# Turning two sets of tiles on TensorE and letting the framework's timeline simulation order the queues, in a hybrid attention and RWKV-7 layer

## The chip, the cores and the metric

The kernel runs on one core of one Trainium2 chip. The time is device microseconds of one execution, the median of several runs. The kernel before took 1992.68 us (three runs, 1992.07 to 1992.70).

## The reference

One layer over 256 tokens and 4096 features, all in float32. A wide projection feeds 16 heads of forgetting attention, 32 heads of RWKV-7 and a gate; one output projection and a LayerNorm follow.

```
proj = x @ w_in                              # 256 x 4096 by 4096 x 16.6k
fox:   p = softmax(q k^T / sqrt(128) + c_t - c_s, causal);  fox_out = p v
rwkv:  S_t = S_{t-1} diag(decay_t) + (S_{t-1} a_t) b_t^T + v_t k_t^T;  y_t = S_t r_t
h   = concat(fox_out, groupnorm(y) * g + b + bonus) * silu(z)
out = LayerNorm(2^(1/4) * x + h @ w_out)
```

## The kernel before

**Projections.** The input projection is cut into 8 groups n of 4 blocks b, each of 512 columns: a group holds two fox heads and two pairs of RWKV heads, the output projection has 8 more blocks of 512 columns. Per block 16 weight tiles w{n}_{b}_{q} of 128x1024 come by DMA. ACT casts each to a rounded upper part (w_qh, L140), DVE subtracts it to get the rest (w_ql, L141), and TensorE multiplies three times per 128 rows of the contraction: L146 and L147 with the upper part, L148 with the rest. One weight tile feeds 12 matmuls of 128x512. In the first and the last weight tile of a block the two accumulators acc{n}_{b}_0 and acc{n}_{b}_1 are filled one behind the other, otherwise in turn. Three such accumulators lie in PSUM, five more PSUM tiles (`pst`) serve everything else. The output projection does the same in L860 to L862.

**Side work.** Everything else is written as generators, each of which runs on to its next `yield` at every `slot()` between projection matmuls. So the program order strews this work among the projections, and `wait(W[...])` says how many slots a generator lets pass. For group n the RWKV generator (`rwkv`) builds BK (the keys and removal vectors per chunk), the small triangular blocks gb and lt, sends the diagonal ones out and loads them back spread over the partitions (nd, Nb), solves them row by row in 31 pairs of DVE instructions (prod L579, xc L582), and then goes over 4 chunks in a chain of small matmuls: rh, copied to R, up, copied to UV by ACT, sp (which reads BKt, the turned BK), added to SV by DVE. The fox generator (`fox`) makes the logits lg, their softmax, turns the probabilities into pT, multiplies them with vt (fop, L744 and L745) and copies that to fo (ACT L747). The two heads of a group use vt{n}, which ACT copies out of the block 1 accumulators (L912), so fop of the odd head has to be done before vt of the next group is written.

**How tiles are turned before.** A 128x128 turn is done in two halves: DVE transposes 32x32 squares in place (STREAM_TRANSPOSE), four DMAs of `turn` (L281) write the tile to DRAM in an order that moves the squares, and one DMA loads it back. BK takes two DVE transposes, four DMAs and one load per group (L547 and `turns`), lg of heads 0 to 13 one DVE transpose, four DMAs and one load. Heads 14 and 15 already have their probabilities turned by three TensorE transposes with the identity (L739) and an ACT copy out of PSUM (L740).

**What sets the order.** The framework's scheduler places all instructions in its queues by priority and readiness. Some have to keep the program's order (`tc.keep_in_program_order`), among them the DMAs of `issue` and some DVE transposes. Engines work their queues strictly in order. At the end of the program the LayerNorm of the first 128 tokens is finished among the last projections of the second 128: zp0 (a transpose of the row factors), eight matmuls wp0_0 to wp0_7 (L1010), each followed by a DVE update of 512 columns (L1011); then the statistics of the second half, mv1 (L979), and its eight updates.

Of the kernel before, what the change touches and what calls it, by code (L numbers as in the profile page):

```python
# [10 lines left out]
F32 = mybir.dt.float32  # L11
# [6 lines left out]
P = 128  # L18
# [3 lines left out]
G = 16  # L22
C = 64
NCH = S // C
# [60 lines left out]
def layer(ctx: ExitStack, tc: tile.TileContext, xt, xtok, w_lora, w_main, muv, w_o, up, par, mulora, fbias, lng, lnb, cst, out):  # L85
    nc = tc.nc
# [8 lines left out]
    def pst(name):  # L95
        return ps.tile([P, 512], F32, tag="ps", name=name)
# [34 lines left out]
    ident = cs[:, C_ID : C_ID + P]  # L131
    ones = cs[:, C_ONES : C_ONES + P]

    def column(name, i):
        return prm[:, PAR.index(name), i : i + 1]
# [21 lines left out]
    for n, (k0, k1) in enumerate(pieces):  # L157
        for k in range(k0, k1):
            t = xpool.tile([P, 2, S], F32R, tag=f"x{k}", name=f"x{k}")
# [31 lines left out]
    def wait(n):  # L191
        for _ in range(n):
            yield
# [67 lines left out]
    rp = mid.enter_context(tc.tile_pool(name="rp", bufs=1))  # L261
# [6 lines left out]
    def t256(tag, name, bufs=1):  # L268
        return rp.tile([P, S], F32, tag=tag, name=name, bufs=bufs)
# [10 lines left out]
    def issue(out, src):  # L280
        tc.keep_in_program_order(nc.sync.dma_start(out=out, in_=src))  # L281

    def turn(src, name, each=2):
        _, m, cols = src.shape
        d = dram.tile([cols // B, B, m, 4, B], F32, tag=f"dt{m}_{cols}", name=name, bufs=2)
        s = src.rearrange("p m (q t) -> p m q t", t=B)
        for a in range(4):
            issue(d[:, :, :, a, :].rearrange("q i m t -> i m q t"), s[B * a : B * (a + 1)])
            if a % each == each - 1:
                yield  # L290
        return d
# [79 lines left out]
    def gate(y, key, k):  # L371
        far = k < FAR
        while len(storing) > 1:
            yield
        h = rp.tile([P, S], F32, tag="h", name=f"h{k}")
        nc.vector.scalar_tensor_tensor(h, y, 0.5, szs[key], ALU.mult, ALU.mult)
        pool, tag, bufs = (rp, "hl", 2) if far else (xpool, f"x{k}", 1)
        hl = pool.tile([P, 2, S], F32R, tag=tag, name=f"hl{k}", bufs=bufs)
        nc.scalar.copy(hl[:, 0, :], h)
        nc.vector.tensor_tensor(hl[:, 1, :], h, hl[:, 0, :].bitcast(F32), ALU.subtract)  # L380
        if far:
            storing.append(k)
            yield from wait(SENT)
            issue(hd[k], flat(hl).bitcast(F32))
            kept_h.add(k)
            storing.remove(k)
        else:
            ht[k] = hl
# [6 lines left out]
    def flat(t):  # L395
        return t.rearrange("p a b -> p (a b)")
# [108 lines left out]
    def rwkv(n):  # L505
# [3 lines left out]
        q = pairs[n]  # L509
        lc, BK, lt, bon = q["lc"], q["BK"], q["lt"], q["bon"]  # L510
# [9 lines left out]
        p, t = bks[n], vs_[n]  # L520
# [22 lines left out]
        SV = [rp.tile([P, 2, NCH, C], F32, tag=f"SV{j}", name=f"SV{j}_{n}") for j in range(2)]  # L543
        UV = [rp.tile([P, 2, NCH, C], F32, tag=f"UV{j}", name=f"UV{j}_{n}") for j in range(2)]
        yield from wait(W["tp"])
        for u in range(2):
            tc.keep_in_program_order(nc.vector.transpose(flat(BK[:, u]), flat(BK[:, u])))  # L547
        yield from wait(W["d1"])
        BKt = rp.tile([P, 2, NCH, P], F32, tag="shl", name=f"BKt{n}")

        def turns():
            d = yield from turn(BK.rearrange("p u c t -> p (u c) t"), f"BKt{n}", 1)
            yield from wait(2)
            issue(BKt.rearrange("p u c t -> p (u c t)"), d.rearrange("q i g a t -> (q i) (g a t)"))
            yield
            vst = UV[0].rearrange("p u c v -> p (u c v)").rearrange("p (m q) -> p m q", m=2)
            for a in range(2):
                tc.keep_in_program_order(nc.vector.transpose(vst[:, a, :], vs_[n][:, a, :]))
            yield from wait(3)
            d = yield from turn(vst, f"vt{n}", 1)  # L560
            yield from wait(2)
            vv[n] = rp.tile([P, 2, S], F32, tag="s2", name=f"vv{n}")
            issue(vv[n], turned_back(d))
            yield from wait(4)
            nc.vector.tensor_tensor(flat(bon), flat(bon), flat(vv[n]), ALU.mult)
            for u in range(2):
                nc.scalar.activation(bon[:, u], bon[:, u], AF.Identity, bias=column("gn_bias", i0 + u))
            bonned.add(n)

        other = turns()  # L570
        prod = rp.tile([P, 2, NJ, B], F32, tag="prod", name=f"prod{n}")
        xc = rp.tile([P, 2, NJ, B], F32, tag="xc", name=f"xc{n}")
# [39 lines left out]
        for u in range(2):  # L612
            for c in range(NCH):
                for j in range(2):
                    a, b = slice(C * j, C * j + B), slice(C * j + B, C * j + C)
# [17 lines left out]
        for u in range(2):  # L633
            for c in range(NCH):
                for j in range(2):
                    a, b = slice(C * j, C * j + B), slice(C * j + B, C * j + C)
                    nc.tensor.matmul(xp[a, u * P + c * B : u * P + (c + 1) * B], Q[b, u, c, :], X[b, u, c, C * j + B : C * j + C], start=True, stop=True)
        for j in range(2):
            a = slice(C * j, C * j + B)
# [67 lines left out]
    def fox(i, q, k, vt):  # L707
        nb = rp.tile([P, 3, P], F32, tag="nb", name=f"nb{i}")
        row = ncd[i : i + 1, :]
        nc.sync.dma_start(out=flat(nb[:, 0:1, :]), in_=row[:, :P].to_broadcast([P, P]))  # L710
        nc.sync.dma_start(out=flat(nb[:, 1:3, :]), in_=row.to_broadcast([P, S]))
        for m in (0, 2):
            nc.gpsimd.affine_select(out=nb[:, m, :], in_=nb[:, m, :], compare_op=ALU.is_ge, fill=NEG, base=0, pattern=[[-1, P]], channel_multiplier=1)
        yield from wait(W["fs"])
        sp = pst(f"fsp{i}")
        nc.tensor.matmul(sp[:, :P], q[:, :P], k[:, :P], start=True, stop=True)
        nc.tensor.matmul(sp[:, P : 3 * P], q[:, P:], k, start=True, stop=True)
        lg = rp.tile([P, 3, P], F32, tag="lg", name=f"lg{i}")
        spv = sp[:, : 3 * P].rearrange("p (a t) -> p a t", t=P)
        st = rp.tile([P, 6], F32, tag="fst", name=f"fst{i}", bufs=2)  # L720
        for m, blk in enumerate((slice(0, 1), slice(1, 3))):
            nc.vector.scalar_tensor_tensor(lg[:, blk, :], spv[:, blk, :], ct[:, m * NF + i : m * NF + i + 1], nb[:, blk, :], ALU.add, ALU.add)
            nc.vector.tensor_reduce(st[:, m : m + 1], lg[:, blk, :], AX.XY, ALU.max, negate=True)
            nc.scalar.activation(lg[:, blk, :], lg[:, blk, :], AF.Exp, bias=st[:, m : m + 1], accum_out=st[:, 2 + m : 3 + m])
            nc.vector.reciprocal(st[:, 4 + m : 5 + m], st[:, 2 + m : 3 + m])
            nc.vector.tensor_scalar(lg[:, blk, :], lg[:, blk, :], st[:, 4 + m : 5 + m], None, ALU.mult)
        if i < G - 2:
            nc.vector.transpose(flat(lg), flat(lg))
        yield from wait(W["fp"])
        if i < G - 2:  # L730
            ld = yield from turn(lg, f"fpt{i}")
            yield
        pT = rp.tile([P, 3 * P], F32, tag="nb", name=f"pT{i}")
        if i < G - 2:
            issue(pT, ld.rearrange("q i m a t -> (q i) (m a t)"))
        else:
            pt = pst(f"fpt{i}")
            for m in range(3):
                nc.tensor.transpose(pt[:, m * P : (m + 1) * P], lg[:, m, :], ident)  # L739
            nc.scalar.copy(pT, pt[:, : 3 * P])  # L740
        yield from wait(W["fo"])
        op = pst(f"fop{i}")
        f = slice(i % 2 * P, i % 2 * P + P)
        nc.tensor.matmul(op[:, :S], vt[:, 0, f], pT[:, :S], start=True, stop=False)  # L744
        nc.tensor.matmul(op[:, P:S], vt[:, 1, f], pT[:, S:], start=False, stop=True)  # L745
        o = t256("fq", f"fo{i}")
        nc.scalar.copy(o, op[:, :S])  # L747
        while f"f{i}" not in szs or 2 * i >= FAR and not closed:
            yield
        yield from gate(o, f"f{i}", 2 * i)  # L750
        foxed.add(i)
# [6 lines left out]
    def chain():  # L758
        while not ff:
            yield  # L760
        yield from forget()
        for n in range(G // 2):
            yield from rwkv(n)
# [5 lines left out]
    def turned_back(d):  # L769
        return d.rearrange("(u b) i m a t -> u (b i) (m a t)", b=4).rearrange("u p s -> p u s")  # L770
# [5 lines left out]
    def unload(n, b, bk, vt):  # L776
# [43 lines left out]
        else:  # L820
# [4 lines left out]
            yield from wait(LAND - 1)  # L825
        nc.scalar.mul(fq, fq, FOX_SCALE)
        side(fox(i, fq, fk, vt))
        yield
        silu2(zf, f"f{i}")
# [89 lines left out]
    for b, q in outs:  # L919
        if q == 0:  # L920
            pool, tag = (ps, "ps") if b == 1 or b and b % 2 == 0 else (pp, "pp")
# [91 lines left out]
    z0, _, last = moments(0)  # L1013
# [79 lines left out]
```

## Time and profile before

| | before |
|---|---|
| median of the runs, us | 1992.68 |
| profiled execution, span, us | 1990.4 |
| TensorE busy, instructions | 1948.0 us, 10063 |
| VectorE busy | 1384.1 us |
| ScalarE busy | 962.3 us |
| DMA, share of 16 engines on the main queue | 72.3% |

The page states the span of the profiled execution and no further time of its own; the runs' median lies 2.28 us above this span, for what comes ahead of the first and behind the last instruction. TensorE is busy 98% of the span, so the time is read from TensorE's gaps and from the pace between them. A timeline row has start, duration, engine, line, operation and, in brackets, how long the engine had been idle before it and what ended the idle time. PEclk is the granted TensorE clock as a share of full speed.

### The profile page before, as it was taken

What the parts mean: (1) busy time and instruction counts of PE and PEld (TensorE: products, weight loads), DVE (VectorE), ACT (ScalarE), POOL (GpSimd) and SP (SyncE); (2) the same over time, 40 slices, a digit from 0 to 9 for tenths busy, and PEclk for the clock granted to TensorE, in tenths of its full rate; (3) what the DMA queues carried; (4) which work ended last, traced back from release to release, by engine and by line L of the source; (5) the groups of instructions that cost most, each with busy time, mean ns of one, the idle gap of its engine ahead of it and who ended that gap; (6) DMA issues with size and microseconds to landing.
All of it is one profiled execution on the core that took longest, in us unless ns stands there. A gap on an engine that the chain in (4) does not pass through costs nothing.

```text
span 1990.4 us, 28153 instructions
## 1 busy us (share of the span) xinstructions
PE 1948.0 (98%) x10063; PEld 1583.7 (80%) x10063; DVE 1384.1 (70%) x2242; ACT 962.3 (48%) x1455; POOL 79.6 (4%) x111
## 2 busy tenths in 40 slices
PE   9998999999999999999999999999999999999998
PEld 8887787788777887778777877787778878888886
DVE  6577658865886588668866886688668856755555
ACT  6552555355535554455355544554455445443333
POOL 0010001000100010001000100010001000000000
PEclk9999999999999999999999999999999999999999
DMA  9577676867786769677867786778676877866664
GB/s 335 150 230 218 196 196 214 237 205 201 224 240 202 211 212 247 201 204 213 251 200 200 219 248 198 201 221 246 197 203 210 262 281 234 259 200 200 196 190 169
DMA packets 328241, 434.03 MB, mean 218 GB/s; under 512 B 198370, under 2 KB 228852, under 8 KB 328100
## 3 DMA queue, kind: packets, MB, share of 16 engines
q1 hardware_dynamic: 327668, 431.81, 72.3%
q8 instruction: 79, 1.29, 0.3%
q14 instruction: 62, 0.51, 0.1%
q10 hardware_dynamic: 432, 0.43, 0.1%
HBM read 395.56 MB, written 36.59 MB: 217 GB/s over the span
## 4 chain that ended last, share of the span: by engine, by line
PE 85%; DVE 11%; issue 2%; ACT 1%; DMA 1%; ACTq 0%; DVEq 0%; SPq 0%
PE acc L146 20%; PE acc L148 20%; PE acc L147 19%; PE oacc L860 6%; PE oacc L861 6%; PE oacc L862 6%; DVE prod L579 3%; DVE xc L582 3%; PE yp L678 1%; PE gp L517 1%; DMA w<-in_w_main_dram 1%; PE up L653 1%; PE rh L626 1%; DVE w_7l L141 1%; DVE w_15l L141 0%
## 5 line engine op out<-in xcount | busy, mean ns | idle before, releaser
L582 DVE TENSOR_REDUCE xc<-prod 128x8 f32<-128x16 f32 (+30 forms) x248 | 72.8, 294 | 7.0
L579 DVE TENSOR_TENSOR prod<-Nb,xc 128x8 f32<-128x8 f32 (+30 forms) x248 | 72.1, 291 | 7.0
L141 DVE TENSOR_TENSOR w_0l<-w,w_0h 128x1024 fp32r<-128x1024 f32 x31 | 37.8, 1220 | 53.0 <-ACT w_0h L140 46.9
L140 ACT CAST w_0h<-w 128x1024 fp32r<-128x1024 f32 x31 | 32.6, 1053 | 74.6 <-DMA w<-in_w_main_dram 63.6
L146 PE MATMUL acc<-w_7h,x 128*128 128x512 f32 x124 | 55.8, 450 | 10.6 <-ACT w_7h L140 10.6
L141 DVE TENSOR_TENSOR w_6l<-w,w_6h 128x1024 fp32r<-128x1024 f32 x31 | 37.9, 1222 | 35.9 <-ACT w_6h L140 19.3
L148 PE MATMUL acc<-w_7l,x 128*128 128x512 f32 x124 | 54.4, 439 | 7.9 <-DVE w_7l L141 7.9
L148 PE MATMUL acc<-w_1l,x 128*128 128x512 f32 x124 | 49.1, 397 | 7.7 <-DVE w_1l L141 7.7
L141 DVE TENSOR_TENSOR w_7l<-w,w_7h 128x1024 fp32r<-128x1024 f32 x31 | 37.9, 1224 | 26.8 <-ACT w_7h L140 16.4
L898 ACT COPY bk<-acc 128x512 f32<-128x512 f32 x48 | 28.0, 586 | 57.8 <-PE acc L148 57.6
L140 ACT CAST w_5h<-w 128x1024 fp32r<-128x1024 f32 x31 | 32.6, 1051 | 46.3 <-PE acc L147 24.5
L147 PE MATMUL acc<-w_7h,x 128*128 128x512 f32 x124 | 53.8, 434 | 0.0
L141 DVE TENSOR_TENSOR w_10l<-w,w_10h 128x1024 fp32r<-128x1024 f32 x31 | 37.9, 1223 | 22.0 <-PE acc L148 18.2
L141 DVE TENSOR_TENSOR w_5l<-w,w_5h 128x1024 fp32r<-128x1024 f32 x31 | 37.9, 1222 | 22.0 <-PE acc L148 13.5
L141 DVE TENSOR_TENSOR w_12l<-w,w_12h 128x1024 fp32r<-128x1024 f32 x31 | 37.5, 1211 | 21.8 <-PE acc L148 9.0
L141 DVE TENSOR_TENSOR w_8l<-w,w_8h 128x1024 fp32r<-128x1024 f32 x31 | 37.7, 1217 | 19.6 <-ACT UV L656 13.5
L141 DVE TENSOR_TENSOR w_11l<-w,w_11h 128x1024 fp32r<-128x1024 f32 x31 | 37.9, 1221 | 19.4 <-PE acc L148 12.0
L146 PE MATMUL acc<-w_15h,x 128*128 128x512 f32 x124 | 49.8, 401 | 1.5 <-ACT w_15h L140 1.5
L146 PE MATMUL acc<-w_8h,x 128*128 128x512 f32 x124 | 50.3, 406 | 0.8 <-ACT w_8h L140 0.8
L146 PE MATMUL acc<-w_9h,x 128*128 128x512 f32 x124 | 49.0, 395 | 1.6 <-ACT w_9h L140 1.6
L146 PE MATMUL acc<-w_5h,x 128*128 128x512 f32 x124 | 50.6, 408 | 0.0
L148 PE MATMUL acc<-w_5l,x 128*128 128x512 f32 x124 | 48.3, 398 | 2.1 <-DVE w_5l L141 2.1
(811 smaller groups left out, 6479.7 us busy)
## 6 DMA issues: line engine op xcount, KB each, us to landing
w<-in_w_main_dram SPq DMA_DIRECT2D x496, 512.0 KB
wo<-in_w_o_dram SPq DMA_DIRECT2D x128, 512.0 KB
bt<-bk SPq DMA_DIRECT2D x88, 128.0 KB
Nb<-nd SPq DMA_DIRECT2D x16, 512.0 KB
wr<-in_w_main_dram SPq DMA_DIRECT2D x15, 512.0 KB
hd<-hl SPq DMA_DIRECT2D x29, 256.0 KB
h<-hd SPq DMA_DIRECT2D x29, 256.0 KB
raw<-bt SPq DMA_DIRECT2D x16, 256.0 KB
```

Source lines behind the costliest of these rows:

```text
L140: nc.scalar.copy(hi[:, :n], src[:, :n])
L141: nc.vector.tensor_tensor(lo[:, :n], src[:, :n], hi[:, :n].bitcast(F32), ALU.subtract)
L146: nc.tensor.matmul(acc[:, :n], xs[k][:, 0, tt], hi[:, o : o + n], start=(k == 0), stop=False)
L147: nc.tensor.matmul(acc[:, :n], xs[k][:, 1, tt], hi[:, o : o + n], start=False, stop=False)
L148: nc.tensor.matmul(acc[:, :n], xs[k][:, 0, tt], lo[:, o : o + n], start=False, stop=(k == KT - 1))
L517: nc.tensor.matmul(gp[u][j][:, c * P : (c + 1) * P], BK[h, u, c, :], lt[j][h, u, c, :], start=True, stop=True)
L579: first = nc.vector.tensor_tensor(prod[:, :, :, s + 1 :], nb[:, :, s : s + 1, s + 1 :].to_broadcast([P, 2, NJ, w]), xc[:, :, :, s + 1 :], ...
L582: nc.vector.tensor_reduce(xc[:, :, :, s : s + 1], prod[:, :, :, s:], AX.X, ALU.add)
L860: nc.tensor.matmul(acc, ht[k][:, 0, tt], hi, start=(k == 0), stop=False)
L861: nc.tensor.matmul(acc, ht[k][:, 1, tt], hi, start=False, stop=False)
L862: nc.tensor.matmul(acc, ht[k][:, 0, tt], lo, start=False, stop=(k == KT - 1))
L898: nc.scalar.copy(bk[:, m, :], acc[m])
```

## The change

Three things change. BK is turned by three TensorE transposes per half u into a PSUM tile bkt, and an ACT copy brings it to BKt: 48 transposes and 16 copies of 128x384 take the place of 16 DVE transposes and 40 DMAs. The probabilities of heads 0 to 13 go the way of heads 14 and 15: 42 transposes and 14 ACT copies in place of 14 DVE transposes and 70 DMAs. And the tile context is told to order the queues by a simulation of time lines.

```diff
@@ rwkv
         yield from wait(W["tp"])
+        BKt = rp.tile([P, 2, NCH - 1, P], F32, tag="shl", name=f"BKt{n}")
         for u in range(2):
-            tc.keep_in_program_order(nc.vector.transpose(flat(BK[:, u]), flat(BK[:, u])))
+            bt = pst(f"bkt{n}_{u}")
+            for c in range(NCH - 1):
+                nc.tensor.transpose(bt[:, c * P : (c + 1) * P], BK[:, u, c, :], ident)
+            nc.scalar.copy(flat(BKt[:, u]), bt[:, : (NCH - 1) * P])
         yield from wait(W["d1"])
-        BKt = rp.tile([P, 2, NCH, P], F32, tag="shl", name=f"BKt{n}")
 
         def turns():
-            d = yield from turn(BK.rearrange("p u c t -> p (u c) t"), f"BKt{n}", 1)
-            yield from wait(2)
-            issue(BKt.rearrange("p u c t -> p (u c t)"), d.rearrange("q i g a t -> (q i) (g a t)"))
-            yield
@@ fox
-        if i < G - 2:
-            nc.vector.transpose(flat(lg), flat(lg))
         yield from wait(W["fp"])
-        if i < G - 2:
-            ld = yield from turn(lg, f"fpt{i}")
-            yield
         pT = rp.tile([P, 3 * P], F32, tag="nb", name=f"pT{i}")
-        if i < G - 2:
-            issue(pT, ld.rearrange("q i m a t -> (q i) (m a t)"))
-        else:
-            pt = pst(f"fpt{i}")
-            for m in range(3):
-                nc.tensor.transpose(pt[:, m * P : (m + 1) * P], lg[:, m, :], ident)
-            nc.scalar.copy(pT, pt[:, : 3 * P])
+        pt = pst(f"fpt{i}")
+        for m in range(3):
+            nc.tensor.transpose(pt[:, m * P : (m + 1) * P], lg[:, m, :], ident)
+        nc.scalar.copy(pT, pt[:, : 3 * P])
@@ kernel
-    with tile.TileContext(nc) as tc:
+    with tile.TileContext(nc, schedule_with_timeline_sim=True) as tc:
```

The third edit moves instructions on every engine. The rows below stand as they are queued; names end in a number that only tells copies apart, and the brackets name the engines and DMA queues whose signals a row waits for.

On TensorE, the place where group 4's third block begins its second accumulator, before the change (fop7, head 7's product, stands 129 rows ahead of it, among the matmuls of w4_1_6, and is not in this piece):

```order
L146 MATMUL acc4_2_0_8512<-w4_2_0h_8467,x1_224 128x512
L147 MATMUL acc4_2_0_8512<-w4_2_0h_8467,x1_224 128x512
L148 MATMUL acc4_2_0_8512<-w4_2_0l_8468,x1_224 128x512
L490 MATMUL np9_8526<-shl9_8452,onesr_831 128x512 [waits PE_49]
L491 MATMUL np9_8526<-shl9_8452,onesr_831 128x512 [waits Activation_49]
L146 MATMUL acc4_2_1_8513<-w4_2_0h_8467,x0_201 128x512 [waits PE_49,Activation_49]
```

The same place of the changed kernel, whose lines L730, L735 and L736 are the transposes and the two parts of fop:

```order
L146 MATMUL acc4_2_0_8504<-w4_2_3h_8533,x6_323 128x512 [waits Activation_49]
L147 MATMUL acc4_2_0_8504<-w4_2_3h_8533,x6_323 128x512
L730 MATMUL fpt7_8126<-cs_72,lg7_8029 128x128 [waits DVE_49,PE_49]
L730 MATMUL fpt7_8126<-cs_72,lg7_8029 128x128 [waits DVE_49]
L730 MATMUL fpt7_8126<-cs_72,lg7_8029 128x128
L735 MATMUL fop7_8160<-pT7_8125,vt3_6712 128x256 [waits Activation_49]
L736 MATMUL fop7_8160<-pT7_8125,vt3_6712 128x128
L146 MATMUL acc4_2_1_8505<-w4_2_0h_8459,x0_201 128x512 [waits PE_49,Activation_49]
```

The transposes, the product that reads their copy and the accumulator that reuses block 1's PSUM now stand in a row; heads 5, 9, 11 and 13 have the same rows. ACT's queue at this place in the changed kernel, with pT and fo (L731, L738), the two copies vt4 that free the accumulator, and hl13, the cast of an earlier gated head:

```order
L731 COPY pT7_8125<-fpt7_8126 128x384 [waits PE_49,Pool_49]
L379 CAST hl13_7891<-h13_7889 128x256 [waits DVE_49]
L738 COPY fo7_8163<-fop7_8160 128x256 [waits PE_49]
L903 COPY vt4_8501<-acc4_1_0_8081 128x256
L903 COPY vt4_8501<-acc4_1_1_8082 128x256
L140 CAST w4_2_4h_8554<-w4_2_4_8506 128x1024 [waits DMAHW3_49,PE_49]
```

For head 5 the two copies into prod3 (L574), which wait for POOL, stand directly ahead of fo5 and vt3. Before the change fo7 stood ahead of hl14 and of the cast w4_1_7h.

On DVE, the beginning of group 4's fourth block before (bk4_2 is turned for the attention inputs, prod and xc are rows of the triangular solve):

```order
L789 STREAM_TRANSPOSE bk4_2_8901<-bk4_2_8901 128x512 [waits Activation_49]
L582 TENSOR_REDUCE xc4_8774<-prod4_8773 128x8 [waits DVE_49]
L579 TENSOR_TENSOR prod4_8773<-Nb4_8639,xc4_8774 128x8x21 [waits DVE_49]
L789 STREAM_TRANSPOSE bk4_2_8901<-bk4_2_8901 128x512 [waits Activation_49]
L582 TENSOR_REDUCE xc4_8774<-prod4_8773 128x8 [waits DVE_49]
L579 TENSOR_TENSOR prod4_8773<-Nb4_8639,xc4_8774 128x8x22 [waits DVE_49]
L141 TENSOR_TENSOR w4_3_1l_8880<-w4_3_1_8830,w4_3_1h_8879 128x1024 [waits DMAHW4_49,PE_49,Activation_49]
```

And in the changed kernel, where gb1 and lt1 are the last triangular blocks, and the first prod waits for the load Nb4:

```order
L141 TENSOR_TENSOR w4_3_1l_8879<-w4_3_1_8830,w4_3_1h_8878 128x1024 [waits DMAHW2_49,PE_49,Activation_49]
L780 STREAM_TRANSPOSE bk4_2_8900<-bk4_2_8900 128x512 [waits Activation_49]
L534 TENSOR_TENSOR gb0_838<-gp4_1_0_8608,cs_72 64x512 [waits PE_49]
L542 TENSOR_TENSOR lt0_4_8239<-gp4_1_0_8608,cs_72 64x512
L534 TENSOR_TENSOR gb1_839<-gp4_1_1_8609,cs_72 64x512 [waits PE_49]
L542 TENSOR_TENSOR lt1_4_8240<-gp4_1_1_8609,cs_72 64x512
L141 TENSOR_TENSOR w4_3_2l_8908<-w4_3_2_8854,w4_3_2h_8907 128x1024 [waits DMAHW3_49,DVE_49,PE_49]
L780 STREAM_TRANSPOSE bk4_2_8900<-bk4_2_8900 128x512 [waits Activation_49]
L141 TENSOR_TENSOR w4_3_3l_8930<-w4_3_3_8876,w4_3_3h_8929 128x1024 [waits DMAHW1_49,DVE_49,PE_49]
L578 TENSOR_TENSOR prod4_8773<-Nb4_8631,xc4_8774 128x8 [waits DMAHW0_49]
L141 TENSOR_TENSOR w4_3_4l_8957<-w4_3_4_8905,w4_3_4h_8956 128x1024 [waits DVE_49,DMAHW2_49,PE_49,Activation_49]
```

Where 28 of the solve's 31 pairs stood ahead of w4_3_4l, one row does now, and this first row stands between two casts. Two more moves, told in words: in the last group the chain from up7_1 to vs7 (about 50 rows of TensorE) stands in one piece behind the first 14 weight tiles of the output's block 0, with only head 15's logits and its three transposes among it, where before it was strewn among those tiles; and at the end all eight wp0 matmuls (L1001, L1010 before) stand behind the last projection, with the eight DVE updates ahead of mv1, where before they alternated with the last 24 projection matmuls.

## The prediction

> **What bounds the kernel now.** I began with the page's busy times.
>
> ```profile
> PE 1948.0 (98%) x10063; PEld 1583.7 (80%) x10063; DVE 1384.1 (70%) x2242; ACT 962.3 (48%) x1455; POOL 79.6 (4%) x111
> ```
>
> TensorE sets the end. Taking work from DVE, or DMAs from the queue, is worth only what TensorE waited for it. So the waits of TensorE come next: total, count, longest.
>
> ```profile
> PE acc L146 <- ACT w_7h L140: 10.6, 7, 2.3
> PE acc L148 <- DVE w_7l L141: 7.9, 8, 4.2
> PE acc L148 <- DVE w_1l L141: 7.7, 8, 1.5
> PE acc L148 <- DVE w_5l L141: 2.1, 7, 0.8
> PE acc L146 <- ACT w_9h L140: 1.6, 1, 1.6
> ```
>
> These five sum to 10.6 + 7.9 + 7.7 + 2.1 + 1.6 = 29.9 us; the first four come once per group, at three places. The timeline of TensorE at one of them, group 3:
>
> ```profile
> 694.70 0.39 PE L146 MATMUL acc<-w_6h,x 128*128 128x512 f32 x1
> 694.93 0.40 PE L147 MATMUL acc<-w_6h,x 128*128 128x512 f32 x1
> ...
> 696.93 0.50 PE L146 MATMUL acc<-w_7h,x 128*128 128x512 f32 x1 [1.38 <-ACT w_7h L140]
> ...
> 698.19 0.50 PE L148 MATMUL acc<-w_7l,x 128*128 128x512 f32 x1 [0.53 <-DVE w_7l L141]
> ...
> 698.90 0.63 PE L147 MATMUL acc<-w_7h,x 128*128 128x512 f32 x1
> 699.33 0.63 PE L148 MATMUL acc<-w_7l,x 128*128 128x512 f32 x1
> ```
>
> Starts lie 0.23 us apart (694.93 less 694.70) and, behind the two waits, 0.43 apart. The windows around it tell why; the column PEclk is the granted clock:
>
> ```profile
> 698.60:702.00 3.40, 3.40 (x10) 2.63 (x9) 3.40 (x8) 2.80 (x5) 0.11 (x1) 0.50 0.70 178
> 576.00:580.00 4.00, 3.04 (x13) 2.18 (x12) 3.90 (x9) 2.10 (x3) 0.00 (x0) 1.00 0.35 64
> 191.70:195.00 3.30, 3.30 (x8) 2.62 (x9) 1.75 (x3) 0.42 (x1) 0.00 (x0) 0.50 0.68 196
> ```
>
> Two waits of 1.38 + 0.53 = 1.91 us close together cost a stretch of 3.4 us at half clock; one wait of about 1 us (576 to 580) does not. (The last row is the first group's stretch.) At half pace 3.4/0.43 = 8 matmuls run where 3.4/0.23 = 15 would: 7 x 0.23 = 1.6 us lost. I count eight of these, one per group, so 12.8 us hang on the waits at w_7h and w_7l beside the waits themselves.
>
> By the Trainium skill (TensorE: Matmul & The Clock Gate, "Why this matters for your kernels") only idle gaps above some 3 us let the clock fall; here 1.91 us in two pieces did, and the measurement decides.
>
> **What the change removes.** Why the w_1l wait exists, on DVE:
>
> ```profile
> 575.34 0.70 DVE L789 STREAM_TRANSPOSE bk<-bk 128x512 f32<-128x512 f32 x1
> ...
> 576.29 0.34 DVE L579 TENSOR_TENSOR prod<-Nb,xc 128x176 f32<-128x176 f32 x1
> 576.55 1.22 DVE L141 TENSOR_TENSOR w_1l<-w,w_1h 128x1024 fp32r<-128x1024 f32 x1
> ```
>
> Transposes and solver rows are queued ahead of the cast. At w_7h it is ACT, which stood behind a product of TensorE and then a gate of DVE:
>
> ```profile
> 694.66 0.37 ACT L747 COPY fo<-fop 128x256 f32<-128x256 f32 x1 [9.80 <-PE fop L745]
> 695.53 0.40 ACT L379 CAST hl<-h 128x256 fp32r<-128x256 f32 x1 [0.49 <-DVE h L376]
> 695.84 1.04 ACT L140 CAST w_7h<-w 128x1024 fp32r<-128x1024 f32 x1
> ```
>
> In the new order the casts stand ahead of both. I take these waits and the windows as gone: **-29.9 - 12.8 = -42.7 us**. The 30 DVE transposes fewer and the 110 DMAs fewer on SP are worth nothing more, since no other wait of TensorE ends on them. The solve comes later in every group, and the chain behind it with it; in groups 0 to 6 projections still lie between its steps, so I price that at 0, and its price where they don't lie there is that of the last group, below.
>
> **The transposes.** Heads 14 and 15 show the price:
>
> ```profile
> 1586.63 0.40 PE L148 MATMUL acc<-w_7l,x 128*128 128x512 f32 x1
> 1586.86 0.49 PE L739 MATMUL fpt<-cs,lg 128*128 128x128 f32 x3
> ...
> 1587.43 0.39 PE L147 MATMUL acc<-w_7h,x 128*128 128x512 f32 x1
> L740 ACT COPY pT<-fpt x2: 481/482/482, 1587.4 to 1645.1; 128x384 f32<-128x384 f32 x2
> ```
>
> From 1586.63 to 1587.43 is 0.80 us, where two projection matmuls take 0.46: three transposes add 0.34. There are 48/3 + 42/3 = 30 such threes: **+10.2 us**. The 30 ACT copies of 0.48 us are 14.5 us on an engine busy 48%: nothing, unless TensorE waits for one, which is next.
>
> The same page ("Part 4: PE-mode transpose") gives about 275 ns for one transpose; 90 of them would be 24.8 us, 14.6 more than the row bears out. It also says that transposes do not count as busy for the clock; at 1586.86 the pace behind them is 0.23, so one group alone does not halve it.
>
> **New waits at the odd heads.** In the new order transposes, pT, fop, fo, vt and the next accumulator form one round trip with nothing between on TensorE. Rows for its steps:
>
> ```profile
> 693.81 0.59 PE L744 MATMUL fop<-pT,vt 128*128 128x256 f32 x2
> ...
> 694.38 0.48 PE L148 MATMUL acc<-w_6l,x 128*128 128x512 f32 x1
> L912 ACT COPY vt<-acc x16: 372/378/382, 119.4 to 1518.7; 128x256 f32<-128x256 f32 x16
> ```
>
> Transposes to the end of pT: 1587.4 less 1586.86 and 0.48, with a signal, 1.1 us. Start of fop to fo: 694.66 - 693.81 = 0.85. Then fo 0.37 and two vt copies, overlapped, 0.65: 1.0. In all 3.0 us, less TensorE's own 0.34 + 0.57 (693.81 to 694.38) = 2.1 us idle. Heads 5, 7, 9, 11, 13: **+10.5 us**. As 2.1 is above the 1.91 that halved the clock, each takes a window of 1.6: **+8.0 us**. If the idle parts, 0.7 and 1.4, fall in different stretches, this is 0.
>
> Head 5 also has ACT waiting for POOL ahead of fo, a wait that no projection stood behind in this way before:
>
> ```profile
> 736.52 0.50 ACT L575 COPY prod<-cs 128x128 f32<-128x128 f32 x2 [4.31 <-POOL vs L522]
> ```
>
> Between 0 and 4.3 us, depending on how late POOL is there; no row is nearer to one end, so I take the middle, **+2.2**.
>
> **The solve's first row.** Ahead of w_4l of each fourth block DVE now waits for the load Nb. Its route, a store and a reload, has this nearest row in the values vs: the copy on ACT, the load's issue on SP, and POOL at its landing.
>
> ```profile
> 726.11 0.36 ACT L896 COPY bk<-acc 128x256 f32<-128x256 f32 x1
> 728.80 0.38 SPq L907 DMA_DIRECT2D vs<-vd  x1
> 732.15 2.10 POOL L521 TENSOR_TENSOR vs<-vs,bk 128x512 f32<-128x512 f32 x1 [11.93 <-DMA vs<-vd]
> ```
>
> From 726.47 to 732.15 is 5.7 us. Between the last gb and the solve the new queue has lt (of gb's size, 0.69, an estimate from its 64x512), two casts of 1.22 and a transpose of 0.70: 3.8 us. So DVE waits 1.9 us, then comes w_4l, and behind it all later casts. The cover is the lead of the casts: one weight tile lasts TensorE 12 x 0.23 = 2.7 us. Ends: 0 if the lead is a whole tile, 1.9 if it is none. As w_1l to w_3l are no longer held up, I lean to the small end: 0.5 x 8 = **+4.0** (0 to 15.2).
>
> **The last group's chain.** Before, projections lay between its steps; now nothing does. Steps by the timelines of TensorE and DVE:
>
> ```profile
> 1631.69 0.46 PE L662 MATMUL sp<-UV,BKt 128*64 128x64 f32 x8
> 1632.20 0.59 DVE L669 TENSOR_TENSOR SV<-sp,sl 64x128 f32<-64x128 f32 x2 [0.50 <-PE sp L662]
> 1633.33 0.45 PE L626 MATMUL rh<-SV,lt 128*64 128x64 f32 x8
> 1633.83 0.29 DVE L628 COPY R<-rh 128x128 f32<-128x128 f32 x1 [1.03 <-PE rh L626]
> 1635.64 0.55 PE L653 MATMUL up<-R,X 128*128 128x64 f32 x4
> 1636.22 0.53 ACT L656 COPY UV<-up 64x128 f32<-64x128 f32 x2 [2.15 <-PE up L653]
> ```
>
> A signal takes 0.05 (the end of rh, 1633.78, to R at 1633.83). So sp to rh takes 0.51 + 0.59 + 0.05 = 1.15, rh to up 0.50 + 0.29 + 0.05 = 0.84, up to the next sp 0.58 + 0.53 + 0.05 = 1.16: 3.2 per round, of which TensorE's own small matmuls fill about half. Two rounds idle 3.2, the last up to yp 0.8, and yp to vs (square, cast, subtraction, 0.60 + 0.63 + 0.69 and two products) 3.6 more, an estimate from before's last group: **+7.6**. Idle this dense takes one window at least: **+1.6**. Bounds 0 (if the reads of the next block fill in) and twice this.
>
> **The end.** Now all eight updates stand between the last projection and mv1:
>
> ```profile
> 1976.73 0.75 DVE L1011 SCALAR_TENSOR_TENSOR res<-res,rs,wp 128x512 f32<-128x512 f32 x1 [0.18 <-PE wp L1010]
> 1977.41 0.69 DVE L871 SCALAR_TENSOR_TENSOR res<-res,oacc 128x512 f32<-128x512 f32 x1
> ```
>
> They follow at 0.68 us: 8 x 0.68 = 5.4, less the eight wp0 that no longer delay projections, 8 x 0.23 = 1.8: **+3.6**.
>
> **The sum** goes against the profiled execution, 1990.4 us of span and 2.3 around it, which is the runs' median of 1992.7: -42.7 + 10.2 + 10.5 + 8.0 + 2.2 + 4.0 + 7.6 + 1.6 + 3.6 = +5.0, so 1997.7, or **1998 us**. Its own range, with the terms that I took between two ends (8.0, 2.2, 4.0, 1.6) moved by half of their sum, is 1990 to 2006.
>
> **Rivals.** *The new waits stay cheap.* It decides where the two halves of each round trip fall into different stretches: then the odd heads' gaps do not halve the clock (-8.0), nor does the chain (-1.6), the lead covers Nb (-4.0) and POOL is early (-2.2): 1982 us, faster. For it: single waits of 1 us left the clock alone, and the halves of the round trip are 0.7 and 1.4. Against: 1.38 and 0.53 sufficed. *The clock needs one long gap.* If gaps near 2 us leave it alone, the old clock term and the new ones vanish together, +12.8 - 9.6: 2001; the row of 0.50 behind 1.38 and 0.53 speaks against it. That is the rule of the Trainium skill quoted above (TensorE: Matmul & The Clock Gate); this trace shows the contrary. *Landings at the queue's head.* The order was fixed by simulated landings; where a real one is later, DVE stands before the casts. From a lead below 1.9 us on, each fourth block loses the full 1.9 (+11.2), and with 1.6 of clock in seven groups as well +11.2 more: 2009 to 2020. *The old waits survive* at half, because the new order doesn't clear their engines: +21.4, 2019; the new rows with nothing ahead of the casts speak against it.
>
> **Chances.** My forecast 0.45, cheap waits 0.27, one long gap 0.02, landings 0.21, old waits 0.05. The range takes in the first and the lower half of the landings: 1980 to 2014. A measurement here tells from no change what exceeds 0.2%, 4 us. Of the forecast's 0.45, 0.03 lies below 1988.7, 0.23 from there to 1996.7, and 0.19 above. So faster 0.27 + 0.03 = 0.30, same 0.23, slower 0.19 + 0.02 + 0.21 + 0.05 = 0.47.
>
> **What would show it.** TensorE's list of waits without w_7h and w_1l, instead acc behind ACT vt and fop behind pT, about 2 us a group; half clock after w_2_3h at odd heads; waits at w_4l; up, sp, rh and vs waited for once. If PEclk reads 1.00 behind the odd heads I am too high; waits for DMA on DVE of more than 2 us a group, and I am too low.

## The result and the profile after

The changed kernel took 2008.14 us (median of four runs, 2005.70 to 2012.57), the kernel before 1992.38 beside it: a ratio of 1.0086, interval 1.0064 to 1.0109. The forecast was 1998, slower. The profiled execution spans 2008.7 us (2010.53 as a run) where before spanned 1990.4: 18.3 us more. So the direction came true, and the working behind it turned out to be wrong in what it credited its largest term to. The page's busy times after:

```profile
PE 1963.2 (98%) x10153; PEld 1598.7 (80%) x10153; DVE 1370.2 (68%) x2212; ACT 980.2 (49%) x1485; POOL 81.0 (4%) x111
```

TensorE's waits after (total, count, longest):

```profile
PE qt L615 <- DMA T<-td: 9.0, 8, 2.8
PE acc L146 <- ACT vt L903: 7.1, 6, 3.4
PE fop L735 <- ACT pT L731: 4.7, 5, 1.0
PE sp L661 <- ACT UV L655: 3.3, 4, 1.1
PE acc L148 <- DVE w_6l L141: 3.1, 2, 2.8
PE vs L691 <- DVE yr L688: 2.8, 1, 2.8
```

None of before's five is left. Six new ones sum to 30.0 us, as many as were there before (29.9). The round trip at an odd head, here head 7, stands as the new order said:

```profile
922.66 0.49 PE L730 MATMUL fpt<-cs,lg 128*128 128x128 f32 x3
924.18 0.70 PE L735 MATMUL fop<-pT,vt 128*128 128x256 f32 x2 [1.03 <-ACT pT L731]
924.72 0.38 PE L736 MATMUL fop<-pT,vt 128*128 128x128 f32 x2
925.84 0.50 PE L146 MATMUL acc<-w_0h,x 128*128 128x512 f32 x1 [0.74 <-ACT vt L903]
```

The second piece of the new time, which I had priced at nothing, is the load T. It is read by the small matmuls qt, here of group 4, which stand among group 5's first projections before it has landed:

```profile
1033.34 0.22 PE L615 MATMUL qt<-T,gb 32*32 32x32 f32 x2 [0.58 <-DMA T<-td]
...
1037.26 0.63 PE L615 MATMUL qt<-T,gb 32*32 32x32 f32 x14 [2.83 <-DMA T<-td]
1037.82 0.80 PE L146 MATMUL acc<-w_6h,x 128*128 128x512 f32 x1
```

The windows behind such waits, again with the granted clock third from the end:

```profile
582.60:586.00 3.40, 3.40 (x9) 2.65 (x9) 3.23 (x13) 2.30 (x3) 0.00 (x0) 0.50 0.71 107
1036.50:1043.30 6.80, 6.04 (x27) 4.82 (x28) 3.76 (x5) 1.41 (x2) 0.00 (x0) 0.50 0.80 247
722.50:729.30 6.80, 5.59 (x13) 4.43 (x14) 1.99 (x4) 3.17 (x8) 2.04 (x5) 0.50 0.47 110
```

The clock halves behind the wait of 2.83 us at w_6l (582.60), behind those for T (1036.50, and from 422.14 to 425.55 behind another wait for T of 2.46 us), and behind head 5's (722.50), whose accumulator waited 3.36 us. Around head 7 it stays at 1.00, although the two waits there sum to 1.77 us, not far from the 1.91 us that halved it before.

The traces show why. The stretches of half clock in this run begin at 422.14, 582.57, 722.51, 1036.54, 1528.06 and 1671.42, among others, and all their distances are whole multiples of 3.413 us: they lie on a fixed grid. On this grid head 7's waits fall into two neighbouring stretches. Head 13's waits, of the same lengths, fall into one, and so do those of group 3 before. Head 7's two stretches, then head 13's and the one that follows it:

```profile
920.49:923.90 3.41, 2.62 (x12) 1.59 (x10) 3.40 (x10) 0.86 (x2) 0.11 (x1) 1.00 0.90 269
923.90:927.31 3.41, 2.39 (x10) 1.91 (x11) 1.03 (x3) 1.56 (x6) 0.00 (x0) 1.00 0.66 223
1524.65:1528.06 3.41, 1.65 (x8) 1.31 (x8) 1.76 (x5) 2.28 (x6) 0.08 (x1) 1.00 0.81 271
1528.06:1531.47 3.41, 3.41 (x10) 2.64 (x9) 1.55 (x1) 0.00 (x0) 2.49 (x2) 0.50 0.66 211
```

And the kernel before, the stretch of group 3's two waits:

```profile
695.16:698.57 3.41, 1.51 (x6) 0.64 (x5) 2.42 (x4) 3.04 (x6) 0.00 (x0) 1.00 0.22 91
```

The number behind the length is TensorE's busy time, so it idles 0.79 and 1.02 us in head 7's stretches, 1.76 in head 13's and 1.90 in that of before. Only behind the last two is the next stretch at half clock.

### The profile page after: what moved, and what is told of

Same layout as the page of the kernel before. It is cut to its first block, busy times and chain, and to the rows that moved or that the text cites. A ratio compares the mean times of both kernels' runs of the same rounds, so it can differ in the third digit from the quotient of the medians.

```text
span 2008.7 us, 28344 instructions
## 1 busy us (share of the span) xinstructions
PE 1963.2 (98%) x10153; PEld 1598.7 (80%) x10153; DVE 1370.2 (68%) x2212; ACT 980.2 (49%) x1485; POOL 81.0 (4%) x111
## 4 chain that ended last, share of the span: by engine, by line
PE 84%; DVE 7%; DMA 4%; ACT 2%; issue 2%; SPq 1%; POOL 0%; ACTq 0%; DVEq 0%; POOLq 0%
PE acc L148 20%; PE acc L146 20%; PE acc L147 19%; PE oacc L851 6%; PE oacc L852 6%; PE oacc L853 6%; DMA td<-xc 1%; PE gp L517 1%; PE yp L677 1%; DMA T<-td 1%; DMA w<-in_w_main_dram 1%; SPq L590 1%; PE up L652 1%; DVE xc L581 1%; PE rh L625 1%
## 5 line engine op out<-in xcount | busy, mean ns | idle before, releaser
L141 DVE TENSOR_TENSOR w_3l<-w,w_3h 128x1024 fp32r<-128x1024 f32 x31 | 41.1, 1326 | 35.5 <-PE acc L148 28.4
L141 DVE TENSOR_TENSOR w_13l<-w,w_13h 128x1024 fp32r<-128x1024 f32 x31 | 37.9, 1223 | 32.6 <-ACT w_13h L140 17.0
L146 PE MATMUL acc<-w_0h,x 128*128 128x512 f32 x124 | 50.4, 406 | 7.1 <-ACT vt L903 7.1
L140 ACT CAST w_4h<-w 128x1024 fp32r<-128x1024 f32 x31 | 32.6, 1053 | 43.8 <-PE acc L147 37.9
L148 PE MATMUL acc<-w_6l,x 128*128 128x512 f32 x124 | 50.2, 408 | 3.1 <-DVE w_6l L141 3.1
L141 DVE TENSOR_TENSOR w_15l<-w,w_15h 128x1024 fp32r<-128x1024 f32 x31 | 37.9, 1222 | 20.1 <-PE acc L148 19.5
L146 PE MATMUL acc<-w_6h,x 128*128 128x512 f32 x124 | 50.4, 407 | 0.0
L141 DVE TENSOR_TENSOR w_5l<-w,w_5h 128x1024 fp32r<-128x1024 f32 x31 | 39.7, 1279 | 15.1 <-issue 7.9
L140 ACT CAST w_12h<-w 128x1024 fp32r<-128x1024 f32 x31 | 32.5, 1048 | 35.7 <-PE acc L147 27.3
L147 PE MATMUL acc<-w_6h,x 128*128 128x512 f32 x124 | 49.8, 401 | 0.0
L148 PE MATMUL acc<-w_8l,x 128*128 128x512 f32 x124 | 49.0, 396 | 0.8 <-DVE w_8l L141 0.8
L148 PE MATMUL acc<-w_2l,x 128*128 128x512 f32 x124 | 48.8, 398 | 0.9 <-DVE w_2l L141 0.7
L146 PE MATMUL acc<-w_1h,x 128*128 128x512 f32 x124 | 49.6, 400 | 0.0
```

Of the source, the lines that this page charges most:

```text
L140: nc.scalar.copy(hi[:, :n], src[:, :n])
L141: nc.vector.tensor_tensor(lo[:, :n], src[:, :n], hi[:, :n].bitcast(F32), ALU.subtract)
L146: nc.tensor.matmul(acc[:, :n], xs[k][:, 0, tt], hi[:, o : o + n], start=(k == 0), stop=False)
L147: nc.tensor.matmul(acc[:, :n], xs[k][:, 1, tt], hi[:, o : o + n], start=False, stop=False)
L148: nc.tensor.matmul(acc[:, :n], xs[k][:, 0, tt], lo[:, o : o + n], start=False, stop=(k == KT - 1))
```

## The experiments

The first question was which of the three edits makes what. My theory at that point (A) was that of the prediction: the turns cost TensorE about 10 us, and the order takes old waits away and puts new ones in their place. The rival (B): the turns are a gain, and the order alone costs.

**Both turns, without the timeline order.**

```diff
-    with tile.TileContext(nc, schedule_with_timeline_sim=True) as tc:
+    with tile.TileContext(nc) as tc:
```

> Both sets of TensorE turns, without the timeline order. Theory A (the 30 threes of transposes cost TensorE 0.34 us each, and the order costs the rest): 1992.4 + 10.2, so 2000 to 2005 us, and the old waits at w_7h, w_7l and w_1l mostly still there. Theory B (the turns are free or a gain, since they take 30 transposes from DVE and 110 DMAs away, and the order alone costs the 16 us): 1985 to 1994 us.

Measured: 1956.39 us, ratio to before 0.9824 (0.9811 to 0.9838). Theory A falls: the turns are a gain of 36 us, larger than B's range allowed, and the timeline order costs 52 on top of them. TensorE's waits in this run:

```profile
PE acc L148 <- DVE w_7l L141: 5.7, 1, 5.7
PE zp L989 <- DVE zd L977: 1.4, 1, 1.4
```

One wait in the first group is all that stays of before's five. A whole group in each of the three kernels, from its first projection matmul to the next group's, and the stretch from the first output projection to the last matmul: length, each engine's busy time, and third from the end the granted clock. Turns alone, group 3 and the last stretch:

```profile
609.50:802.90 193.40, 193.40 (x1047) 158.30 (x1046) 140.64 (x239) 100.62 (x157) 10.77 (x12) 1.00 0.74 211
1579.50:1948.30 368.80, 367.08 (x1759) 301.35 (x1752) 221.19 (x261) 156.77 (x198) 4.70 (x8) 1.00 0.67 206
```

The kernel before, the same two:

```profile
619.60:817.50 197.90, 194.82 (x1035) 157.99 (x1034) 143.45 (x244) 98.35 (x154) 9.63 (x12) 0.99 0.75 217
1614.30:1984.50 370.20, 368.50 (x1753) 302.02 (x1751) 223.05 (x262) 158.14 (x197) 4.71 (x8) 1.00 0.65 212
```

The changed kernel, the same two:

```profile
612.60:816.30 203.70, 197.68 (x1047) 160.30 (x1046) 141.75 (x242) 101.37 (x157) 7.32 (x12) 0.98 0.70 201
1619.80:2003.00 383.20, 374.99 (x1785) 306.39 (x1783) 222.83 (x269) 158.22 (x199) 4.05 (x6) 0.98 0.65 198
```

With turns alone TensorE is busy through all 193.4 us, at full clock, transposes included. Before needed 197.9, of which 3.1 were waits (1.38, 0.53, 0.96 and 0.21) and 1.6 the half clock: without these 193.2. The twelve transposes of this group cost about what was forecast: by the starts of the matmuls around them they add 0.34, 0.66 (six in a row) and 0.12 + 0.23 us, together 1.35. So the old waits had cost more than their own length and the half clock, by about 1 us a group. A part of that shows: the start behind the matmul that ends a wait comes 0.33 us later (696.93 to 697.26 before), where others come after 0.23. With the timeline order groups 2 to 7 take 197.9 to 204.7 us each, and the last stretch 14.4 us more than with turns alone. Over the whole span TensorE idles 45.5 us in the changed kernel (2008.7 less 1963.2 busy) and 18.4 with turns alone (1955.1 less 1936.7). The granted clock is 0.50 for 42.5 us and for 8.9; half of the difference, less what falls into idle time, is a loss of some 16 us more, an estimate. These two make some 43 of the 53.6 us between the two profiled spans.

**The order alone, and each turn alone.** The first is the kernel before with the third edit only, the next two have the first or the second edit only.

```diff
-    with tile.TileContext(nc) as tc:
+    with tile.TileContext(nc, schedule_with_timeline_sim=True) as tc:
```

> The kernel before with the timeline order alone. Theory A: the old waits of 30 us go, about as much comes back as waits for T, vt and the last chain: 1993 to 2000 us, with fop no longer waiting for pT from ACT. Theory B: 2005 to 2012 us, all of the loss.

Measured: 2109.36 us, 1.0588 (1.0572 to 1.0604). This is 117 us slower than before and far above both ranges, with one wait in front:

```profile
PE fop L744 <- DMA pT<-fpt: 83.7, 13, 15.1
PE acc L146 <- ACT vt L912: 13.7, 7, 2.5
PE acc L148 <- DVE w_2l L141: 6.0, 4, 1.5
```

The timeline order puts fop directly ahead of the accumulator here too, while pT still comes back through DRAM; TensorE stands up to 15.1 us for it. Of the old waits those at w_7h and w_1l are no longer in this run's list either, and w_7l is down to 3.1 us in two: the order clears these casts by itself too, but TensorE then waits at others (w_2l above, w_10l 3.7 us, w_4l 2.6).

BK's edit alone, without the order (and the rest of `rwkv` as in the change):

```diff
-            tc.keep_in_program_order(nc.vector.transpose(flat(BK[:, u]), flat(BK[:, u])))
+            bt = pst(f"bkt{n}_{u}")
+            for c in range(NCH - 1):
+                nc.tensor.transpose(bt[:, c * P : (c + 1) * P], BK[:, u, c, :], ident)
+            nc.scalar.copy(flat(BKt[:, u]), bt[:, : (NCH - 1) * P])
```

> Only BK turned on TensorE, old order. Theory A: 16 threes x 0.34 = +5.4 us if the other waits stay, so about 1998. Theory B: 1985 to 1994, since 16 DVE transposes and 40 DMAs leave the queues that the solve uses.

Measured: 1980.91 us, 0.9946 (0.9934 to 0.9959), below both ranges. The waits at w_1l and w_5l are gone, those at w_7h and w_7l stay:

```profile
PE acc L146 <- ACT w_7h L140: 10.6, 7, 2.3
PE acc L148 <- DVE w_7l L141: 9.4, 8, 5.7
```

DVE's rows show what moved: in groups 1 to 6 the cast w_1l comes behind 22 of the solve's 31 prod rows before and behind 17 here, w_5l behind 31 and behind 24. Why the scheduler then places fewer solver rows ahead of them isn't shown.

The probabilities' edit alone:

```diff
-        if i < G - 2:
-            nc.vector.transpose(flat(lg), flat(lg))
...
+        for m in range(3):
+            nc.tensor.transpose(pt[:, m * P : (m + 1) * P], lg[:, m, :], ident)
+        nc.scalar.copy(pT, pt[:, : 3 * P])
```

> Only the probabilities turned on TensorE, old order. Theory A: 14 threes x 0.34 = +4.8 us, about 1997. Theory B: 1985 to 1994: 70 DMAs and 14 DVE transposes fewer shorten the wait of ACT for fop, and with it the one at w_7h.

Measured: 1967.29 us, 0.9879 (0.9865 to 0.9892), again below both ranges. Now the other pair is gone, but for the first group's wait at w_7l:

```profile
PE acc L148 <- DVE w_1l L141: 7.2, 7, 1.5
PE acc L148 <- DVE w_7l L141: 4.2, 1, 4.2
PE acc L148 <- DVE w_5l L141: 2.2, 7, 1.0
```

Each turn takes away its own wait: 11.9 and 25.5 us in time, 37.4 together, and both together gave 36.4. The bigger one includes the windows at half clock. In the queue of ACT fo7 and hl14 still stand ahead of w4_1_7h when both turns are in; what moved is fop7 on TensorE. Between it and the first matmul of w4_1_7h lie 4 rows before and 48 here; of the two edits it is that of the probabilities which does it, the one that takes pT off the way through DRAM. ACT in turns alone, at head 7:

```profile
867.79 0.36 ACT L738 COPY fo<-fop 128x256 f32<-128x256 f32 x1
870.25 1.06 ACT L140 CAST w_7h<-w 128x1024 fp32r<-128x1024 f32 x1 [1.12 <-PE acc L147]
```

The copy fo, which had ACT wait 9.80 us before, is not waited for, and w_7h is done at 871.31, 7 us ahead of its first matmul at 878.43.

**What of the order costs the 52 us.** Theory C: the round trips at the odd heads; D: something else. First the round trip made without the order, by holding the generators of the odd heads from 5 on back by 60 slots (head 15's too):

```diff
-        yield from wait(W["fp"])
+        yield from wait(W["fp"] + (60 if i % 2 and i > 4 else 0))
```

> Both turns, old scheduler, and heads 5, 7, 9, 11 and 13 made to transpose 55 slots later, so that transposes, pT, fop, fo and vt stand in one piece ahead of the next block's second accumulator, as in the changed kernel. Theory C (such a round trip costs what the changed kernel shows, 1.03 + 0.74 = 1.8 us idle, and sometimes a window at half clock): 1956.4 + 5 x 1.8 = 1965, and up to 8 more with the clock. Theory D (the round trips are hidden, the loss of the timeline order lies elsewhere): 1955 to 1959.

Measured: 2013.27 us, 1.0110 (1.0090 to 1.0129). Neither: the loss is 57 us. Because the program then runs all side work in one go until the head is done, the solve's preparation got squeezed too:

```profile
PE bkt L550 <- POOL BK L519: 15.2, 5, 3.2
PE acc L148 <- DVE w_7l L141: 5.8, 1, 5.8
PE qt L615 <- DMA T<-td: 4.8, 6, 1.4
PE acc L146 <- ACT vt L903: 3.7, 5, 0.7
```

The accumulator's part, 0.7 per head, is that of the changed kernel (0.74), as nothing stands between fop and the accumulator here either; but the run does not tell C from D. In the next run that generator alone is held back and stepped:

```diff
         yield from wait(W["fp"])
+        while i in (5, 7, 9, 11, 13) and i not in due:
+            yield
...
+                for _ in range(12):
+                    if n and 2 * n - 1 not in foxed:
+                        try:
+                            next(foxg[2 * n - 1])
+                        except StopIteration:
+                            sides.remove(foxg[2 * n - 1])
```

> Both turns, old scheduler; for heads 5, 7, 9, 11 and 13 only the attention generator is held back until the block is done, so the rest of the side work stays where it is. Between the transposes and fop the old scheduler puts six projection rows, between fop and the next accumulator four. If the loss at the odd heads comes from standing with nothing between, this costs nearly nothing: 1955 to 1959. If it comes from being late at all, 5 x 1.8 us and some clock: 1963 to 1972. In the run that held back all side work the five groups each grew by 11 us.

Measured: 1955.25 us, 0.9807 (0.9792 to 0.9822): no loss against turns alone. TensorE waits for neither pT nor vt; its two longest waits:

```profile
PE acc L148 <- DVE w_7l L141: 5.7, 1, 5.7
PE zp L1002 <- DVE zd L990: 1.4, 1, 1.4
```

So the heads may come as late as that. Six projection rows between transposes and fop, and four rows between fop and the accumulator, are cover enough; with none, the changed kernel pays 1.77 us a head (1.03 and 0.74).

**Only some engines under the timeline order.** Every DVE instruction (then every ACT instruction too) kept behind the one traced before it, the rest as in the change:

```diff
+    def vin(op, *args, **kw):
+        return tc.keep_in_program_order(getattr(nc.vector, op)(*args, **kw))
...
-            nc.vector.tensor_reduce(xc[:, :, :, s : s + 1], prod[:, :, :, s:], AX.X, ALU.add)
+            vin("tensor_reduce", xc[:, :, :, s : s + 1], prod[:, :, :, s:], AX.X, ALU.add)
```

> The changed kernel with every DVE instruction kept behind the one traced before it, so that the timeline order works on the other engines alone. If the order of DVE (the solve late and among the casts) is what costs the 52 us between turns alone and turns with the timeline order, 1955 to 1970. If it is the order of TensorE or ACT in itself, still 1990 to 2010.

> As the run before, with ACT kept in program order too; TensorE and the DMA queue are still ordered by the timeline simulation. If the order of DVE and ACT makes all of the loss: within 5 us of 1956. If TensorE's own order has a part: that part above 1956.

Measured: 2212.88 us (1.1111, 1.1088 to 1.1135) and 2232.73 us (1.1213, 1.1186 to 1.1240). Both expectations missed: program order on DVE is much worse than either scheduler's, so these runs say nothing on the 52 us. DVE stands there for steps of the chain; its longest wait in the first of the two runs, 7.6 us in all with turns alone:

```profile
DVE SV L99 <- PE sp L664: 108.5, 23, 7.6
```

**The order with one turn.** The change without BK's edit, then without the probabilities':

> Probabilities turned on TensorE, BK by DVE and DMAs, timeline order. The timeline order alone took 2109, with fop waiting 83.7 us for the load of pT; with pT from TensorE these waits should shrink to the 4.7 us that the changed kernel shows, so about 2109 - 79 - 15 of clock = 2015. If instead the turn of BK is what saved the changed kernel, 2060 to 2110.

Measured: 2049.68 us, 1.0300 (1.0274 to 1.0326), 35 us above the first expectation and below the second. The wait for pT by DMA is gone as thought, but against the changed kernel's 7.1 and 9.0 us vt and T grew:

```profile
PE acc L146 <- ACT vt L904: 17.0, 6, 3.4
PE qt L616 <- DMA T<-td: 11.5, 14, 2.5
```

> BK turned on TensorE, probabilities by DVE and DMAs, timeline order. If the loss of the timeline order alone (117 us) is the wait of fop for the load of pT, BK's turn helps it little: 2090 to 2110. If the DMAs of BK made pT late, below 2060.

Measured: 2100.93 us, 1.0538 (1.0517 to 1.0558), as expected: fop's wait for the load stays, and with it the loss.

```profile
PE fop L743 <- DMA pT<-fpt: 69.3, 8, 10.5
```

**The wait for T by itself.** The changed kernel with more slots ahead of the reads of T:

```diff
-W = {"fo": 3, "vs": 2, "np": 4, "gp": 5, "tp": 4, "d1": 8, "d2": 12, "xp": 3, "fs": 4, "fp": 5}
+W = {"fo": 3, "vs": 2, "np": 4, "gp": 5, "tp": 4, "d1": 8, "d2": 24, "xp": 3, "fs": 4, "fp": 5}
```

> The changed kernel with the slots ahead of the X turns and qt (which read the load T) raised from 12 to 24. If qt's wait for T (9.0 us and about three windows at half clock) is a part of the loss that can be taken away alone, 2008 - 9 - 5 = 1994. If the timeline order puts other work into the same stall, within 5 us of 2008 or above.

Measured: 2052.44 us, 1.0292 (1.0272 to 1.0312). The wait for T halved, and the timeline order made another of it:

```profile
PE acc L146 <- ACT vt L903: 29.6, 4, 11.5
PE sp L661 <- ACT UV L655: 5.3, 4, 2.4
PE qt L615 <- DMA T<-td: 4.3, 5, 1.2
```

So this term could not be taken away by a later slot; the order was made anew.

**The version that the runs point to.** Both turns, the old scheduler, and the one wait that is left (w_7l, behind 13 pairs of solver rows in the first group) taken away by keeping every fourth solver row of that group behind what was traced before it:

```diff
-            if not t:
+            if not t or not n and t % 4 == 0:
                 tc.keep_in_program_order(first)
```

> Both turns, old scheduler, and in the first group every fourth solver row kept behind what was traced before it on DVE, so that the cast w_7l no longer stands behind 13 pairs of solver rows. Turns alone waits 5.7 us there and runs 6.8 us at half clock: 1956.4 - 5.7 - 1.6 to 3 = 1948 to 1950 if the wait goes, 1956 if another takes its place.

Measured: 1948.70 us, 0.9772 (0.9757 to 0.9787), 2.3% faster than before, and 59 us less than the change's 2008.14. TensorE's longest waits are now at the two ends of the program:

```profile
PE zp L989 <- DVE zd L977: 1.4, 1, 1.4
PE warmup L108 <- POOL idle L105: 1.3, 1, 1.3
```

## Why the prediction was right in its direction and wrong in its working

- **The old waits, -42.7.** The waits did go, and the size was about right (before ran nine stretches at half clock in these places and not eight, two of them in the first group, from 189.99 to 196.81), but the step that credits them to the order failed, and with it "The 30 DVE transposes fewer and the 110 DMAs fewer on SP are worth nothing more". The waits go without the order too (1956.39): BK's turn removes its pair (w_1l, w_5l), the probabilities' turn the other (w_7h, w_7l; the first group's wait at w_7l stays). "In the new order the casts stand ahead of both" is true of the rows, and the order alone does clear w_7h and w_1l; but it puts other waits in their place and has no saving to show, at 2109.36. I did not ask whether the casts would still be late in the old order once the transposes and the round trip through DRAM were gone.
- **The transposes, +10.2.** Right: in group 3 of turns alone twelve of them add 1.35 us, four times 0.34 is 1.36. The record of one lasts 0.27 us, but in the stream it adds 0.11. The saving beside them was larger than thought: 36.4 us net of the transposes, where 42.7 - 10.2 = 32.5 had been forecast.
- **The odd heads, +10.5.** fop 4.7 and vt 7.1 are 11.8 us, of which 3.4 fell on the accumulator behind head 5, so head 5's extra 2.2 is in it: 12.7 expected for both. Right.
- **Their half clock, +8.0.** The condition set beside this term decided it: where the idle parts fall into different stretches, there is no loss. They did at heads 7 and 9. At head 11 they left 1.51 us in one stretch, with the clock at 1.00 behind it; at head 13 1.76 us, with 3.4 us at 0.50 behind it; and behind head 5's longer wait it was 6.8 us. That is three stretches where I had five, 4.8 us at the 1.6 of the forecast.
- **The solve's first row, +4.0.** In seven of the eight groups DVE did stand for a load ahead of the first row, six times 1.9 to 4.4 us (Nb) where I had 1.9, and once 7.6 (the profile names fq). Only the last cost TensorE more than 1 us, at w_6l (2.8 us) and not w_4l, with a window of 3.4 us at half clock; elsewhere the lead of the casts covered it. Waits of DVE for DMA above 2 us a group were the sign that I had named for being too low.
- **The last group's chain, +7.6 + 1.6, and the end, +3.6.** The last stretch took 383.2 us against 370.2 before: 13.0 for 12.8 expected. The chain's part, in the longest waits among its rows; behind them the clock stood at 0.50 from 1671.42 to 1681.66, three stretches where I had one:

```profile
1664.75 0.46 PE L661 MATMUL sp<-UV,BKt 128*64 128x64 f32 x8 [1.12 <-ACT UV L655]
...
1666.00 0.45 PE L625 MATMUL rh<-SV,lt 128*64 128x64 f32 x8 [0.44 <-DVE SV L668]
...
1676.21 0.77 PE L691 MATMUL vs<-yr,onesr 128*128 128x512 f32 x1 [2.75 <-DVE yr L688]
```

- **What was missing:** the later solve at "so I price that at 0". qt's waits for T are 9.0 us, and neither before nor with turns alone does TensorE wait for T. Three stretches at half clock follow the two longest (one behind 2.46 us, two behind 2.83), 4.8 us at the forecast's 1.6. Together 13.8 us, this is more than the 10 us between 1998 and 2008.

The rule of one long gap (the Trainium skill, TensorE: Matmul & The Clock Gate, "Why this matters for your kernels") was set aside rightly: 1.90 us in two pieces within one stretch halved the clock before, 1.76 us did at head 13. That section of the Trainium skill advises against gaps above some 3 us; that only such gaps count was my reading of it. Head 7's 1.77 us are no exception, since they lie in two stretches. The runs don't show the exact limit: 1.51 us in one stretch left the clock alone at head 11.

That the sum came near was luck in part: a saving credited to the order and 4 us too small (36.4 us, from the turns) stood against a cost that I had put 14 us too low (37.5 us for the order, 52 measured on top of the turns).

What stays open: how the 52 us divide among the places of the order. Idle time and half clock account for some 43 of them, as given above, but no run took one place's share away. Each attempt to take one term away under the timeline order produced another order; only the round trips were made separately, in the old order, and there they cost nothing as soon as a few rows lay between.

## What to carry to other kernels

When a change has an edit that moves everything and one that does not, price the small one alone first: by what it removes from the queues as they stand, and only then the new order. A wait of the busiest engine on a cast can have its cause two engines away (here a load through DRAM, then a product, then a copy ahead of the cast), and an edit that shortens that chain can be worth more than the busy time that it frees. A dependency chain across engines may need only a little cover, here four to six rows of TensorE; an order that left none between its steps cost more than lateness did.

## What the runs showed of the hardware that was not expected

Half clock came in stretches of 3.4 us or multiples of it (3.4 at 582.60, 6.8 at 722.50 and 1036.50), and in each run they all begin on one grid of 3.413 us. What counted was the idle time within one stretch of this grid, and not the sum of two waits that stand close together: 1.90 us (before, 695.16 to 698.57) and 1.76 (after, 1524.65 to 1528.06) halved the clock of the next stretch, and 1.77 us spread over two stretches (after, 920.49 to 927.31) did not. Idle time does not tell all: with BK's turn alone 1.64 us in one stretch halved the clock once (692.11) and once did not (1480.59).
